# Forget heads' bias by a running sum on VectorE, and 84 matmuls of the unit matrix ahead of the first products

## The chip, the cores and the metric

The kernel runs on one core of one Trainium2 chip. The metric is the time of one execution on the device, in microseconds (us). In what follows PE is TensorE, DVE is VectorE, ACT is ScalarE, POOL is GpSimd and SP is SyncE, whose queue issues most of the DMAs.

## The reference, cut to what matters

One layer mixes 512 tokens of width 2048 through three branches of four heads of 128 channels: A (forgetting attention), B (attention in chunks with a learned bias) and C (stick-breaking attention). Their outputs are gated, projected up, weighted by merge gates, summed and projected out. The change touches branch A:

```python
def forgetting_attention(q, k, v, f_logit):
    log_f = jax.nn.log_sigmoid(f_logit.astype(jnp.float32))
    c = jnp.cumsum(log_f, axis=1).transpose(0, 2, 1)          # (b, heads, tokens)
    for i in range(nb):                                       # blocks of 128 queries
        logits = einsum('bhqd,bhkd->bhqk', q[lo:hi], k[:hi]) * scale
        logits = logits + c[:, :, lo:hi, None] - c[:, :, None, :hi]
        logits = jnp.where(mask, logits, NEG)
        p = jax.nn.softmax(logits, axis=-1)
        outs.append(einsum('bhqk,bhkd->bhqd', p, v[:, :, :hi]))
```

The term `c[query]` is the same for all keys of a row, so a softmax over keys does not depend on it; the term `-c[key]` does matter.

## The kernel before, in words

Activations lie transposed: 128 channels on the partitions, 512 tokens along the row. Every product of float32 operands is made from float32r parts. A weight tile is split by `prep` into a rounded part `wh` (ACT, line 243) and a rest `wl` (DVE, line 247), and `mm` (line 262) multiplies both with the split activations.

The work is a list of units, each one weight tile of 128x1024 (later 128x768). The units come in this order: the first head of branch C through `first_quad`, which takes Q, K, V, G and the forget logits together while x is still being normalised; gate columns; then the heads C1 to C3, B0 to B3, A0 to A3, each with two seven-product tasks for Q/K and V/G and one or two for gate columns; then the up projection (`up_units`) and the output projection (`out_pair`). From the up to the output projection the merged tiles must be combined: `merged_a` and `merged_b` make `m1`, `m2`, `mt`, `mu` and their splits `m23`, `m4` on DVE and ACT.

The order of instructions on PE, ACT and DVE is fixed when the kernel is built. A planner, `Flow`, runs all tasks as generators; each says which engine it wants and for how long, and the planner picks by earliest start and due time. So a task with other costs or other buffers can move instructions of its neighbours. On the chip each engine then works through its own list in order. Weights are fetched by SP (line 274) into six `raw` tiles; sums of weight tiles come by POOL's queue (line 278).

Branch A before. `forget_bias` computes log f of all four heads as a 128x16 tile and stores it to a DRAM tile `fd2`. `forget_sums`, run shortly before A0, loads it four times, makes the running sum over 512 tokens on DVE (`fs`), splits it, and assembles two tiles: `crl` and `crb`, in which rows of the sum and rows of ones stand so that a matmul of the two gives c[query] - c[key]. For each A head, `soft_start` makes `cr` by an ACT copy of `crb` with the mask `ohf` as scale (line 956), and `soft_scores` adds it to the scores in PSUM with one matmul per query block (line 980, 128 to 512 columns). Then a bf16 matmul of the unit matrix `identb` with the mask `mska` adds the causal mask (line 981), DVE takes the maximum (line 984), ACT the exponential straight from PSUM (line 986).

Branch B before. The bias of a head is a tile `tb`, fetched by SP in `soft_start`. DVE adds it to the scores, writes them to SBUF and takes the maximum in one instruction (line 991), reads the maximum out and negates it (line 993); ACT takes the exponential in SBUF (line 996).

At the start of the program PE has nothing to do until x and the first weight tile are loaded and split. `identb` is made early (POOL line 307, DVE line 310).

Of the kernel before, what the change touches and what calls it, by code (L numbers as in the profile page):

```python
# [15 lines left out]
P = 128  # L16
S = 512
# [10 lines left out]
HS = S // 2  # L28
EPS = 1e-6
NEG = -1e30  # L30
SCALE = HD ** -0.5
LA = 2

# [29 lines left out]
class Flow:  # L63
# [16 lines left out]
    def give(self, slots, n=1):  # L80
        slots.free += [self.fin] * n
# [67 lines left out]
def mm_us(n, x=1):  # L149
    return x * max(0.115, n / 2400 + 0.0133)  # L150


def act_us(n, x=1):
    return x * (0.075 + 0.00095 * n)


def dve_us(n, x=1):
    return x * (0.1 + 0.00105 * n)
# [3 lines left out]
def hybrid_kernel(  # L162
# [34 lines left out]
    def t2(s, dt=F32):  # L197
        return tp.tile([P, S], dt, tag="t2", name=nm(s))
# [11 lines left out]
    def f(ap):  # L210
        return ap.bitcast(F32)

    def blk(i):
        return slice(i * P, (i + 1) * P)
# [22 lines left out]
    def pair_of(name, dt=F32R):  # L237
        return t2(name + "h", dt), t2(name + "l", dt)

    def split(hi, lo, src, n, ev=None, due=(), hi_ev=None):  # L240

        yield (ACT, act_us(n), *due)
        nc.scalar.activation(hi, src, AF.Copy)  # L243
        if hi_ev is not None:
            set_(hi_ev)
        yield (DVE, dve_us(n), *due)
        nc.vector.tensor_sub(lo, src, f(hi))  # L247
        if ev is not None:
            set_(ev)
# [23 lines left out]
    def fetch(to, src, ready, kb):  # L273
        nc.sync.dma_start(to, src)
        return Event(landing(ready, kb))
# [42 lines left out]
    nc.gpsimd.affine_select(out=mskc, in_=zerof, pattern=[[-1, P]], base=0, channel_multiplier=1,  # L318
                            compare_op=ALU.is_gt, fill=NEG)

    ohf = cp.tile([P, NH], F32, name="ohf")
    nc.gpsimd.memset(ohf, 0.0)
    for r in range(4):
        nc.gpsimd.affine_select(out=ohf[32 * r:32 * r + 32, :], in_=ohf[32 * r:32 * r + 32, :],
                                pattern=[[1, NH]], base=0, channel_multiplier=-1,
                                compare_op=ALU.not_equal, fill=1.0)

    gq = cp.tile([P, 4], F32, name="gq")
    nc.vector.tensor_copy(gq, gqk)
    for c in (0, 2):  # L330
# [16 lines left out]
    def at(u, g):  # L347
        side.setdefault(u, []).append(g)
# [56 lines left out]
    xraw, x_in = [None] * KT, [Event() for _ in range(KT)]  # L405
    first_ps = att()
    atts.free.pop()
    xps.free.clear()


# [383 lines left out]

    gl = {}
    yd = {}
    bias, bias_ev, f_ev, f2_ev = {}, Event(), Event(), Event()
    fd, fd2 = dp.tile([2 * NH, S], F32, name="fd"), dp.tile([NH, S], F32, name="fd2")

    def forget_bias():  # L800

        T = S // 32
        lf = cp.tile([P, 4 * T], F32, name="lf")
        v, u, s, p = (lf[:, i * T:(i + 1) * T] for i in range(4))
        yield f_ev
        nc.sync.dma_start(v, fd[:NH, :].rearrange("h (c t) -> (h c) t", t=T))
        nc.sync.dma_start(u, fd[NH:, :].rearrange("h (c t) -> (h c) t", t=T))
        yield Event(f_ev.t + 6.0)
        q = 0.15
        yield DVE, q  # L810
        nc.vector.scalar_tensor_tensor(v, v, bfc, u, op0=ALU.add, op1=ALU.add)
        yield DVE, q
        nc.vector.scalar_tensor_tensor(u, v, -1.0, v, op0=ALU.mult, op1=ALU.min)
        yield ACT, q
        nc.scalar.activation(u, u, AF.Exp)

        yield DVE, 5 * q
        nc.vector.tensor_scalar_add(s, u, 2.0)
        nc.vector.reciprocal(s, s)
        nc.vector.tensor_mul(s, s, u)  # L820
        nc.vector.tensor_mul(u, s, s)
        nc.vector.tensor_scalar_mul(p, u, 1.0 / 17.0)
        for k in range(7, 0, -1):
            yield DVE, q
            nc.vector.scalar_tensor_tensor(p, p, 1.0 / (2 * k + 1), u, op0=ALU.add, op1=ALU.mult)
        yield DVE, 3 * q
        nc.vector.scalar_tensor_tensor(p, p, 1.0, s, op0=ALU.add, op1=ALU.mult)
        nc.vector.tensor_scalar_mul(p, p, 2.0)
        nc.vector.scalar_tensor_tensor(v, v, 0.0, p, op0=ALU.min, op1=ALU.subtract)
        nc.sync.dma_start(fd2.rearrange("h (c t) -> (h c) t", t=T), v)  # L830
        f2_ev.t = flow.fin + 3.0

    def forget_sums():
        yield f2_ev
        yield t2s, 3
        v, s, u = t2("fv"), t2("fs"), t2("fu")
        nc.gpsimd.memset(v, 0.0)
        nc.gpsimd.memset(u, 1.0)
        for r in range(4):
            nc.sync.dma_start(v[32 * r:32 * r + NH, :], fd2)  # L840
        yield Event(flow.now + 6.0)
        yield DVE, 1.2
        nc.vector.tensor_tensor_scan(s, u, v, 0.0, op0=ALU.mult, op1=ALU.add)
        give(t2s)
        yield t2s, 2
        hi, lo = pair_of("c")
        yield from split(hi, lo, s, S)
        give(t2s)
        yield t2s, 2
        crl, crb = t2("crl", F32R), t2("crb")  # L850
        a = ACT, act_us(S)
        yield a
        nc.scalar.activation(crl[0:32, :], f(hi[0:32, :]), AF.Copy)
        yield a
        nc.scalar.activation(crl[32:64, :], f(lo[32:64, :]), AF.Copy)
        yield a
        nc.scalar.activation(crl[64:128, :], u[64:128, :], AF.Copy)
        nc.gpsimd.memset(crb[0:64, :], 1.0)
        yield a
        nc.scalar.activation(crb[64:96, :], f(hi[64:96, :]), AF.Copy, scale=-1.0)  # L860
        yield a
        nc.scalar.activation(crb[96:128, :], f(lo[96:128, :]), AF.Copy, scale=-1.0)
        give(t2s, 3)
        bias["crl"], bias["crb"] = crl, crb
        set_(bias_ev)

    def tri(name, dt=F32):

# [5 lines left out]
    class Head:  # L874
# [73 lines left out]
        def soft_start(self):  # L948
            n = self.n
            yield from self.turn()  # L950
            yield t2s, 4
            if n == A:
                yield bias_ev
                self.bias = t2("cr", F32R)
                yield ACT, act_us(S)
                nc.scalar.activation(self.bias, bias["crb"], AF.Copy, scale=ohf[:, self.h:self.h + 1])
                set_(self.event("b"))
            else:
                self.bias = t2("tb")
                ev = fetch(self.bias, rel[self.h], flow.now, 256)  # L960
                yield ev
                yield DVE, 0.15
                nc.vector.memset(self.bias[0:64, S - 64:], NEG)
                set_(self.event("b"))
            self.p = tri("p")[::-1]

        def soft_scores(self, i):
            n = self.n
            m = (i + 1) * P
            for e in (("p", Q), ("p", K), ("b",)):  # L970
                yield self.event(*e)
            yield atts, 1
            (qh, ql), (kh, kl) = self.c[Q], self.c[K]
            yield PE, mm_us(m, 3) + (mm_us(m) + mm_us(P) if n == A else 0)
            ps = att()[:, :m]
            mm3(ps, qh[:, blk(i)], ql[:, blk(i)], kh[:, :m], kl[:, :m], True, n == B)
            p = self.p[i]
            mx, sm = small("mx"), small("sm")
            if n == A:
                nc.tensor.matmul(ps, bias["crl"][:, blk(i)], self.bias[:, :m], start=False, stop=False)  # L980
                nc.tensor.matmul(ps[:, blk(i)], identb, mska, start=False, stop=True)
                done = self.nth("s", QB)
                yield DVE, dve_us(m)
                nc.vector.tensor_reduce(mx, ps, axis=AX.X, op=ALU.max, negate=True)
                yield ACT, act_us(m) + 0.25
                nc.scalar.activation(p, ps, AF.Exp, bias=mx, accum_out=sm)
                give(atts)
            else:
                done = self.nth("s", QB)
                yield DVE, dve_us(m) + 0.15  # L990
                nc.vector.tensor_tensor_reduce(out=p, in0=ps, in1=self.bias[:, S - m:], scale=1.0,
                                               scalar=-3e38, op0=ALU.add, op1=ALU.max, accum_out=mx)
                nc.vector.tensor_scalar_mul(mx, mx, -1.0)
                give(atts)
                yield ACT, act_us(m) + 0.25
                nc.scalar.activation(p, p, AF.Exp, bias=mx, accum_out=sm)
            if done:
                give(t2s, 5)
            yield DVE, 0.16
            nc.vector.reciprocal(sm, sm)  # L1000
            yield ACT, act_us(m) + 0.1
            nc.scalar.activation(p, p, AF.Copy, scale=sm)
            set_(self.event("s", i))
# [273 lines left out]

    first_head(C, 0)
    for n, h in [(C, 1), (C, 2), (C, 3)] + [(n, h) for n in (B, A) for h in range(NH)]:
        if (n, h) == (A, 0):  # L1280
            at(len(units) - 4, forget_sums)
        last_head = head(n, h, (n, h) == (A, NH - 1))


# [304 lines left out]
```

## Time and profile before

| | |
|---|---|
| median of 3 runs | 1350.9 us (1350.63 to 1351.42) |
| the profiled execution's own time | 1351.01 us |
| its span, first to last instruction | 1349.3 us, so 1.7 us lie around it |
| busy share of the span | PE 98%, weight load 85%, DVE 82%, ACT 59%, POOL 7% |
| chain that ended last | PE 96%, DVE 3% |

How to read it: the span is cut into the time in which each engine ran something. PE's matmuls overlap, so the time that one takes from its neighbours is read from start to start and not from its own duration. A row of a timeline has the start, the duration, the engine, the line, the operation, out<-in, shapes and a count; a bracket behind it gives the time that the engine was idle before it and what ended that.

### The profile page before, as it was taken

What the parts mean: (1) busy time and instruction counts of PE and PEld (TensorE: products, weight loads), DVE (VectorE), ACT (ScalarE), POOL (GpSimd) and SP (SyncE); (2) the same over time, 40 slices, a digit from 0 to 9 for tenths busy, and PEclk for the clock granted to TensorE, in tenths of its full rate; (3) what the DMA queues carried; (4) which work ended last, traced back from release to release, by engine and by line L of the source; (5) the groups of instructions that cost most, each with busy time, mean ns of one, the idle gap of its engine ahead of it and who ended that gap; (6) DMA issues with size and microseconds to landing.
All of it is one profiled execution on the core that took longest, in us unless ns stands there. A gap on an engine that the chain in (4) does not pass through costs nothing.

```text
span 1349.3 us, 19660 instructions
## 1 busy us (share of the span) xinstructions
PE 1326.0 (98%) x7338; PEld 1149.2 (85%) x7338; DVE 1108.8 (82%) x1589; ACT 797.3 (59%) x1224; POOL 93.5 (7%) x123
## 2 busy tenths in 40 slices
PE   7999999999999999999999999999999999989998
PEld 5788888888888888888888888888888788878887
DVE  5998998978878788787888878878787877898786
ACT  6755756656565576655767557665567645454443
POOL 0000000010000000000110000100000000000000
PEclk9999999999999999999999999999999999989999
DMA  9556766667767677777777777777767655758893
GB/s 327 173 143 157 194 171 181 187 195 194 187 196 202 183 212 183 187 204 183 212 174 190 193 194 196 167 193 186 192 184 250 246 192 179 209 134 245 236 250 89
DMA packets 91055, 262.00 MB, mean 194 GB/s; under 512 B 10168, under 2 KB 16440, under 8 KB 90960
## 3 DMA queue, kind: packets, MB, share of 16 engines
q1 hardware_dynamic: 72384, 201.96, 44.6%
q0 software_dynamic: 14976, 54.53, 24.7%
q10 hardware_dynamic: 3600, 4.26, 0.9%
q8 instruction: 57, 0.93, 0.3%
q14 instruction: 38, 0.31, 0.1%
HBM read 241.03 MB, written 19.69 MB: 193 GB/s over the span
## 4 chain that ended last, share of the span: by engine, by line
PE 96%; DVE 3%; DMA 0%; issue 0%; ACT 0%; SPq 0%; DVEq 0%; ACTq 0%
PE acc L262 82%; PE att L262 8%; PE att L1013 1%; DVE wl L247 1%; DVE m L247 1%; PE att L1116 1%; PE att L258 1%; PE att L1117 1%; PE att L259 1%; PE att L257 1%; PE att L1115 1%; DMA x<-in_xT 0%; PE att L1076 0%; PE att L911 0%; PE att L912 0%
## 5 line engine op out<-in xcount | busy, mean ns | idle before, releaser
L247 DVE TENSOR_TENSOR wl<-raw,wh 128x1024 fp32r<-128x1024 f32 (+1 forms) x412 | 494.2, 1200 | 149.7 <-ACT wh L243 148.8
L243 ACT ACTIVATE wh<-raw 128x1024 fp32r<-128x1024 f32 (+1 forms) x412 | 427.1, 1038 | 149.8 <-PE acc L262 69.5
L262 PE MATMUL acc<-x,wh 128*128 128x512 f32 x1600 | 416.1, 396 | 10.0 <-ACT wh L243 10.0
L262 PEld LDWEIGHTS acc<-x,wh 128*128 128x128 f32 x1600 | 287.0, 189 | 62.0 <-ACT wh L243 10.0
L262 PE MATMUL acc<-t,wh 128*128 128x512 f32 x1056 | 272.7, 395 | 0.2 <-ACT wh L243 0.2
L262 PEld LDWEIGHTS acc<-x,wl 128*128 128x128 f32 x1504 | 210.6, 190 | 18.9
L262 PE MATMUL acc<-x,wl 128*128 128x256 f32 (+1 forms) x1504 | 223.7, 289 | 0.0
L262 PEld LDWEIGHTS acc<-t,wh 128*128 128x128 f32 x1056 | 188.0, 189 | 31.9 <-ACT wh L243 0.4
L262 PEld LDWEIGHTS acc<-t,wl 128*128 128x128 f32 x1056 | 145.0, 190 | 11.0
L262 PE MATMUL acc<-t,wl 128*128 128x256 f32 x1056 | 148.6, 282 | 0.0
L278 POOL DMA_DIRECT2D raw<-in_w_col x88 | 76.1, 865 | 934.7 <-DMA raw<-in_w_col 429.1
L262 PE MATMUL acc<-m,wh 128*128 128x512 f32 x448 | 113.8, 396 | 6.4 <-DVE m L247 6.0
L262 PEld LDWEIGHTS acc<-m,wh 128*128 128x128 f32 x448 | 81.6, 191 | 21.6 <-DVE m L247 6.4
L746 ACT ACTIVATE c<-acc 128x256 f32<-128x256 f32 x50 | 19.2, 384 | 105.4 <-PE acc L262 100.4
L724 ACT ACTIVATE u<-acc 128x512 f32<-128x512 f32 x50 | 29.8, 596 | 66.6 <-PE acc L262 66.5
L262 PE MATMUL att<-y,wh 128*128 128x512 f32 x256 | 66.5, 391 | 1.3 <-DVE y L247 1.3
L262 PEld LDWEIGHTS acc<-m,wl 128*128 128x128 f32 x448 | 61.9, 193 | 5.1 <-DVE wl L247 0.8
L636 DVE TENSOR_TENSOR raw<-raw,raw 128x1024 f32<-128x1024 f32 x52 | 63.5, 1221 | 0.4
L630 DVE TENSOR_TENSOR raw<-raw,raw 128x1024 f32<-128x1024 f32 x52 | 63.4, 1220 | 0.4
L262 PE MATMUL acc<-m,wl 128*128 128x256 f32 x448 | 63.4, 285 | 0.4 <-DVE wl L247 0.4
L707 ACT ACTIVATE v<-acc 128x512 f32<-128x512 f32 x52 | 31.1, 599 | 49.4 <-PE acc L262 46.1
L262 PEld LDWEIGHTS att<-y,wh 128*128 128x128 f32 x256 | 47.9, 188 | 12.2 <-DVE y L247 2.5
(193 smaller groups left out, 1371.9 us busy)
## 6 DMA issues: line engine op xcount, KB each, us to landing
raw<-in_w_col SPq DMA_DIRECT2D x236, 512.0 KB, 4.4
raw<-in_w_col POOLq DMA_DIRECT2D x88, 512.0 KB, 6.4
raw<-in_w_out SPq DMA_DIRECT2D x40, 512.0 KB, 4.4
gl<-c SPq DMA_DIRECT2D x48, 256.0 KB, 2.2
raw<-in_w_up SPq DMA_DIRECT2D x32, 384.0 KB, 3.1
sg<-gl SPq DMA_DIRECT2D x48, 256.0 KB, 5.1
raw<-in_w_out POOLq DMA_DIRECT2D x16, 512.0 KB, 6.8
x<-in_xT SPq DMA_DIRECT2D x16, 256.0 KB, 7.0
```

Of the source, the lines that this page charges most:

```text
L243: nc.scalar.activation(hi, src, AF.Copy)
L247: nc.vector.tensor_sub(lo, src, f(hi))
L257: nc.tensor.matmul(ps, lh, rh, start=start, stop=False, skip_group_check=more)
L258: nc.tensor.matmul(ps, lh, rl, start=False, stop=False, skip_group_check=more)
L259: nc.tensor.matmul(ps, ll, rh, start=False, stop=stop, skip_group_check=more)
L262: nc.tensor.matmul(ps, w, x, start=start, stop=stop, skip_group_check=more)
L278: nc.gpsimd.dma_start(to, src, accum_op=ALU.add)
L630: nc.vector.tensor_add(w[1], w[1], w[5])
L636: nc.vector.tensor_add(w[2], w[2], w[1])
L707: nc.scalar.activation(self.v, ps, AF.Copy)
L724: nc.scalar.activation(self.u, ps, AF.Copy)
L746: nc.scalar.activation(c, ps[:, RH], AF.Copy, scale=-1.0)
```

## The change

It does two things. First, the forget heads take their bias as branch B does. `forget_bias` stores -log f (one more DVE instruction of 128x16); `forget_sums`, the mask `ohf`, the tiles `crl` and `crb` and the matmul of line 980 are gone. Each A head fetches its row of `fd2` to all 128 partitions (256 KB on SP's queue) into `cr`, and DVE makes the running sum in place (128x512). Each query block is then treated as in B: DVE adds the bias, writes to SBUF and takes the maximum; ACT takes the exponential in SBUF. The mask matmul stays. Second, 84 matmuls of `identb` with itself (128x128, bf16) into the PSUM tile `first_ps` stand ahead of the first product; their result is overwritten.

```diff
+WARM = 84
...
-    ohf = cp.tile([P, NH], F32, name="ohf")
-    nc.gpsimd.memset(ohf, 0.0)
-    for r in range(4):
-        nc.gpsimd.affine_select(out=ohf[32 * r:32 * r + 32, :], in_=ohf[32 * r:32 * r + 32, :],
...
     first_ps = att()
     atts.free.pop()
+    for _ in range(WARM):
+        nc.tensor.matmul(first_ps[:, :P], identb, identb, start=True, stop=True)
...
-        nc.vector.scalar_tensor_tensor(v, v, 0.0, p, op0=ALU.min, op1=ALU.subtract)
+        nc.vector.tensor_scalar(v, v, -1.0, 0.0, op0=ALU.mult, op1=ALU.max)
+        nc.vector.tensor_add(v, v, p)
...
-    def forget_sums():
...
             if n == A:
-                yield bias_ev
-                self.bias = t2("cr", F32R)
-                yield ACT, act_us(S)
-                nc.scalar.activation(self.bias, bias["crb"], AF.Copy, scale=ohf[:, self.h:self.h + 1])
+                yield f2_ev
+                b = self.bias = t2("cr")
+                ev = fetch(b, fd2[self.h:self.h + 1, :].to_broadcast([P, S]), flow.now, 256)
+                yield ev
+                yield DVE, dve_us(2 * S)
+                nc.vector.tensor_tensor_scan(b, b, b, 0.0, op0=ALU.add, op1=ALU.max)
...
             if n == A:
-                nc.tensor.matmul(ps, bias["crl"][:, blk(i)], self.bias[:, :m], start=False, stop=False)
                 nc.tensor.matmul(ps[:, blk(i)], identb, mska, start=False, stop=True)
-                done = self.nth("s", QB)
-                yield DVE, dve_us(m)
-                nc.vector.tensor_reduce(mx, ps, axis=AX.X, op=ALU.max, negate=True)
-                yield ACT, act_us(m) + 0.25
-                nc.scalar.activation(p, ps, AF.Exp, bias=mx, accum_out=sm)
-                give(atts)
-            else:
...
+            done = self.nth("s", QB)
+            yield DVE, dve_us(m) + 0.15
+            b = self.bias[:, :m] if n == A else self.bias[:, S - m:]
+            nc.vector.tensor_tensor_reduce(out=p, in0=ps, in1=b, scale=1.0, scalar=-3e38, op0=ALU.add, op1=ALU.max,
+                                           accum_out=mx)
+            nc.vector.tensor_scalar_mul(mx, mx, -1.0)
+            give(atts)
+            yield ACT, act_us(m) + 0.25
+            nc.scalar.activation(p, p, AF.Exp, bias=mx, accum_out=sm)
...
-        if (n, h) == (A, 0):
-            at(len(units) - 4, forget_sums)
```

Line numbers in rows of the changed kernel differ from those of the kernel before: line 247 becomes 248, 253 becomes 254, 262 becomes 263, 1370 becomes 1326 and 1377 becomes 1333.

The planner moves instructions at three places that the prediction speaks of. The first is the start of PE's list; `acc_224`, `att_226` and so on are the PSUM tiles of the first head, `x_2` the first x tile. Before:

```order
L1584 UNCONDITIONAL_BRANCH
L262 MATMUL acc_224<-x_2_126,wh_214 128x512
L262 MATMUL acc_225<-x_2_126,wh_214 128x512
L262 MATMUL att_226<-x_2_126,wh_214 128x512
L262 MATMUL att_227<-x_2_126,wh_214 128x512
L262 MATMUL att_142<-x_2_126,w_121 8x512
```

With the change, where the pair of lines 403 stands 84 times:

```order
L403 LDWEIGHTS identb
L403 MATMUL att_128<-identb 128x128
L263 MATMUL acc_294<-x_2_112,wh_284 128x512
L263 MATMUL acc_295<-x_2_112,wh_284 128x512
L263 MATMUL att_296<-x_2_112,wh_284 128x512
```

The 84 pairs wait for `identb` alone and stand ahead of everything else on PE; what follows is unchanged.

The second place is DVE at the first scores of A0. `qkl` is the rest of the normalised queries or keys, `wl` that of a weight tile, `att_7580` the PSUM tile of the first scores. Before:

```order
L247 TENSOR_TENSOR qkl_7533<-rs_7342,qkh_7532 128x512
L247 TENSOR_TENSOR wl_7549<-raw_7304,wh_7548 128x1024
L984 TENSOR_REDUCE mx_7584<-att_7580 128x1
L247 TENSOR_TENSOR wl_7575<-raw_7378,wh_7574 128x1024
L1000 RECIPROCAL sm_7585<-sm_7585 128x1
```

With the change:

```order
L248 TENSOR_TENSOR qkl_7579<-rs_7391,qkh_7578 128x512
L248 TENSOR_TENSOR wl_7595<-raw_7353,wh_7594 128x1024
L921 SCALAR_TENSOR_TENSOR cr_7562<-cr_7562 128x512
L248 TENSOR_TENSOR wl_7621<-raw_7427,wh_7620 128x1024
L949 ISA p_7631,mx_7650<-att_7646,cr_7562 128x128
L949 ISA mx_7650 128x1
L951 TENSOR_SCALAR mx_7650<-mx_7650 128x1
```

The running sum (line 921) stands where the first maximum stood, and the next weight split is queued behind it; the first scores come one weight split later, on PE six to sixteen matmuls later. In the other A heads it is the same, in A3 the sum stands ahead of the last `qkl`.

The third place is DVE at the end of the up projection, where `sg` are the gated products, `mt` and `mu` the combinations of merged tiles 6 and 14 (numbers 11567 and 11611 before, 11620 and 11621 after), `m` the splits. Before:

```order
L247 TENSOR_TENSOR m_2108_11612<-sg_11379,m_2108_11612 128x2x256
L253 SCALAR_TENSOR_TENSOR mt_11567<-sg_11379,sg_11307 128x256
L1370 TENSOR_TENSOR sg_11463<-att_11596,sg_11463 128x512
L1377 TENSOR_TENSOR sg_11449<-sg_11449,sg_11463 128x512
L247 TENSOR_TENSOR wl_11620<-raw_11469,wh_11619 128x1024
L253 SCALAR_TENSOR_TENSOR mt_11567<-mt_11567,sg_11307 128x256
L630 TENSOR_TENSOR raw_11469<-raw_11469,raw_11432 128x1024
L1370 TENSOR_TENSOR sg_11518<-acc_11621,sg_11518 128x512
L1396 TENSOR_TENSOR sg_11449<-sg_11449 128x256
L253 SCALAR_TENSOR_TENSOR mu_11611<-mt_11567,sg_11379 128x256
```

With the change:

```order
L248 TENSOR_TENSOR m_2095_11622<-sg_11432,m_2095_11622 128x2x256
L1326 TENSOR_TENSOR sg_11502<-acc_11610,sg_11502 128x512
L254 SCALAR_TENSOR_TENSOR mt_11620<-sg_11432,sg_11360 128x256
L254 SCALAR_TENSOR_TENSOR mt_11620<-mt_11620,sg_11360 128x256
L254 SCALAR_TENSOR_TENSOR mu_11621<-mt_11620,sg_11432 128x256
L248 TENSOR_TENSOR wl_11647<-raw_11449,wh_11646 128x768
L1326 TENSOR_TENSOR sg_11504<-att_11635,sg_11504 128x512
L1333 TENSOR_TENSOR sg_11502<-sg_11502,sg_11504 128x512
L1326 TENSOR_TENSOR sg_11506<-att_11657,sg_11506 128x512
L1333 TENSOR_TENSOR sg_11502<-sg_11502,sg_11506 128x512
```

The three combinations `mt`, `mt`, `mu` now stand together and earlier: all three are ahead of the last two `sg` of that block, where before only the first was. The instructions between there and the last `m23` split are otherwise the same.

More of the change, by code (lines that the diff above doesn't have):

```diff
@@ L319, in hybrid_kernel @@
                             compare_op=ALU.is_gt, fill=NEG)
-    ohf = cp.tile([P, NH], F32, name="ohf")
-    nc.gpsimd.memset(ohf, 0.0)
-    for r in range(4):
-        nc.gpsimd.affine_select(out=ohf[32 * r:32 * r + 32, :], in_=ohf[32 * r:32 * r + 32, :],
-                                pattern=[[1, NH]], base=0, channel_multiplier=-1,
-                                compare_op=ALU.not_equal, fill=1.0)
     gq = cp.tile([P, 4], F32, name="gq")
@@ L796, in hybrid_kernel @@
     yd = {}
-    bias, bias_ev, f_ev, f2_ev = {}, Event(), Event(), Event()
+    f_ev, f2_ev = Event(), Event()
     fd, fd2 = dp.tile([2 * NH, S], F32, name="fd"), dp.tile([NH, S], F32, name="fd2")
@@ L825, in forget_bias @@
             nc.vector.scalar_tensor_tensor(p, p, 1.0 / (2 * k + 1), u, op0=ALU.add, op1=ALU.mult)
-        yield DVE, 3 * q
+        yield DVE, 4 * q
         nc.vector.scalar_tensor_tensor(p, p, 1.0, s, op0=ALU.add, op1=ALU.mult)
         nc.vector.tensor_scalar_mul(p, p, 2.0)
-        nc.vector.scalar_tensor_tensor(v, v, 0.0, p, op0=ALU.min, op1=ALU.subtract)
+        nc.vector.tensor_scalar(v, v, -1.0, 0.0, op0=ALU.mult, op1=ALU.max)
+        nc.vector.tensor_add(v, v, p)
         nc.sync.dma_start(fd2.rearrange("h (c t) -> (h c) t", t=T), v)
         f2_ev.t = flow.fin + 3.0
-    def forget_sums():
[L834 to L865, printed above, removed]
     def tri(name, dt=F32):
@@ L973, in soft_scores @@
             (qh, ql), (kh, kl) = self.c[Q], self.c[K]
-            yield PE, mm_us(m, 3) + (mm_us(m) + mm_us(P) if n == A else 0)
+            yield PE, mm_us(m, 3) + (mm_us(P) if n == A else 0)
             ps = att()[:, :m]
@@ L979, in soft_scores @@
             if n == A:
-                nc.tensor.matmul(ps, bias["crl"][:, blk(i)], self.bias[:, :m], start=False, stop=False)
                 nc.tensor.matmul(ps[:, blk(i)], identb, mska, start=False, stop=True)
-                done = self.nth("s", QB)
-                yield DVE, dve_us(m)
-                nc.vector.tensor_reduce(mx, ps, axis=AX.X, op=ALU.max, negate=True)
-                yield ACT, act_us(m) + 0.25
-                nc.scalar.activation(p, ps, AF.Exp, bias=mx, accum_out=sm)
-                give(atts)
-            else:
[L989 to L996, printed above, removed]
+            done = self.nth("s", QB)
[7 more added lines that the diff above has]
+            nc.scalar.activation(p, p, AF.Exp, bias=mx, accum_out=sm)
             if done:
```

## Prediction

> **What bounds the kernel now.** I read the page's first and fourth part, then PE's waits, then the chain, then the timeline where the change acts.
>
> ```profile
> PE 1326.0 (98%) x7338; PEld 1149.2 (85%) x7338; DVE 1108.8 (82%) x1589; ACT 797.3 (59%) x1224; POOL 93.5 (7%) x123
> ```
> ```profile
> PE 96%; DVE 3%; DMA 0%; issue 0%; ACT 0%; SPq 0%; DVEq 0%; ACTq 0%
> ```
> ```profile
> PE acc L262 <- ACT wh L243: 10.6, 3, 10.0
> PE acc L262 <- DVE m L247: 6.0, 1, 6.0
> PE att L262 <- DVE y L247: 1.3, 2, 1.0
> ```
>
> PE is the bound. It idles 10.0 us before its first matmul, 6.0 us once for a split `m`, 1.3 us for a `y`, and hardly anywhere else. So whatever is taken off PE between the start and the end counts in full, and work on DVE or ACT counts only where PE waits for it. Two windows inside the heads of B and the first of A show the cover:
>
> ```profile
> 539.00:623.00 84.00, 84.00 (x489) 74.02 (x488) 68.78 (x99) 52.64 (x79) 6.91 (x8) 1.00 0.73 193
> 623.00:711.00 88.00, 88.00 (x512) 77.56 (x511) 72.72 (x104) 56.81 (x86) 8.43 (x11) 1.00 0.74 191
> ```
>
> The columns are the length, then the busy time of PE, PEld, DVE, ACT and POOL, the granted clock, the DMA share and GB/s. PE has no idle time in either, DVE is free for 15 us of each.
>
> **Part one, the first products.** PE's first pieces in the chain (start, length, line, count), and what they wait for:
>
> ```profile
> 8.96 0.95 ACT wh L243
> 9.96 1.22 PE acc L262 x2
> 11.19 1.28 PE att L262 x3
> 12.46 0.85 PE acc L262 x2
> 13.32 1.28 PE att L262 x3
> 15.06 0.70 PE att L262 x3
> ```
> ```profile
> 1.66 0.29 DVE L310 CAST identb<-identf 128x128 bf16<-128x128 f32 x1 [0.32 <-POOL identf L307]
> ```
>
> The first ten matmuls of 512 columns run at 1.28/3 = 0.43 us each, later ones at 0.70/3 = 0.23. That is half speed. The page's granted clock says 1.00 there, but the trace has the same picture with the clock beside it after PE's one long wait:
>
> ```profile
> 1195.60:1198.00 2.40, 0.00 (x0) 0.00 (x0) 2.40 (x8) 1.05 (x2) 0.86 (x1) 0.50 0.70 183
> 1198.00:1202.20 4.20, 4.16 (x14) 3.68 (x15) 1.88 (x4) 1.06 (x1) 0.00 (x0) 0.50 0.97 216
> ```
>
> The granted clock is 0.50 while PE idles and for another 4.2 us of work. At the start the slow stretch is as long, from 9.96 to about 14.4. So after some 4.4 us of matmuls the clock is free. If PE has done that before 9.96, the ten matmuls cost 10 x 0.23 and not 10 x 0.43: a gain of 2.0 us. It stays, since PE then runs without a wait to 198 us in this trace, and the DVE's work there follows PE.
>
> What the 84 cost: the nearest rows are the mask matmul of the same type (line 981) and its neighbours.
>
> ```profile
> 756.01 0.28 PE L259 MATMUL att<-qkh,qkl 128*128 128x128 f32 x1
> 756.13 0.27 PE L980 MATMUL att<-cr,crl 128*128 128x128 f32 x1
> 756.24 0.23 PE L981 MATMUL att<-mska,identb 128*128 128x128 bf16 x1
> 756.28 1.40 PE L262 MATMUL acc<-t,wh 128*128 128x512 f32 x5
> ```
> ```profile
> L980 PEld LDWEIGHTS att<-cr,crl 128*128 128x128 f32 x16 | 3.0, 189 | 0.2
> L981 PEld LDWEIGHTS <-identb 128*128 128x128 bf16 x16 | 1.5, 96 | 1.9 <-issue 1.7
> ```
>
> A float32r matmul of 128 columns takes 0.11 us from start to start, the bf16 one 0.04; its weight load lasts half as long (96 against 189 ns). Between 0.04 and 0.11 I take 0.06, half of the float32r one, since weights of 128 columns set that pace and load in half the time. At half clock I double it. `identb` is there at 1.95. In 4.4 slow us 4.4/0.12 = 37 are done, the other 47 take 2.8: the end is at 9.1, before the 9.96 of the first split. At 0.04 it is 7.5; at 0.11 20 are done slowly, 64 take 7.0, and the end is at 13.4: 3.4 us too late, a net loss of 1.4. So this part lies between -2.0 and +1.4, and I take -2.0. [...]
>
> **Part two, the bias matmul.** From the row at 756.13 it costs 0.11 for 128 columns; the other end of its sizes:
>
> ```profile
> 1015.41 0.39 PE L980 MATMUL att<-cr,crl 128*128 128x512 f32 x1
> 1015.64 0.23 PE L981 MATMUL att<-mska,identb 128*128 128x128 bf16 x1
> ```
>
> 0.23 for 512. The sizes 256 and 384 lie between; with 0.12 to 0.15 and 0.17 to 0.19 a head saves 0.63 to 0.68. Four heads: 2.5 to 2.7, I take -2.6. All of it is on PE's path.
>
> What is added for it: per A head one running sum, four reads of the maximum and four negations on DVE, and one DMA on SP. The sum of 512 is priced by the scan of branch C:
>
> ```profile
> L1060 DVE TENSOR_TENSOR_SCAN lk<-lk 128x512 f32<-128x512 f32 x4 | 4.9, 1219 | 0.0
> ```
>
> That is 1.2 us, the reads and negations are what B heads already carry in the window 539 to 623, where 15 us of DVE are free and PE does not idle; so the sum is hidden there, and I cost it at nothing. If that cover were gone it would be 4 x 1.2. The removed `forget_sums` (ACT, DVE, POOL, four DMAs) lies in the window 623 to 711, where PE does not wait either: nothing. The exponential from SBUF instead of PSUM is ACT's, off the path. The mask matmul stays, so its 0.04 stay.
>
> The DMA `cr` adds a wait: DVE's sum waits for its landing, and behind it stand the weight split and the first maximum of that head. Cover: SP issues it where it now issues the gate columns ahead of A0, and the sum stands behind the weight split at 754:
>
> ```profile
> DMA to landing us min/median/max: 6.9/6.9/6.9
> ```
> ```profile
> 742.55 3.53 SPq L1156 DMA_DIRECT2D gl<-c  x2
> ```
> ```profile
> 754.13 1.22 DVE L247 TENSOR_TENSOR wl<-raw,wh 128x1024 fp32r<-128x1024 f32 x1 [0.83 <-ACT wh L243]
> ```
>
> The first row is that of B's `tb`, also 256 KB. Issued at 746.1, `cr` would land at 753.0; DVE gets there at 755.3. That is 2.3 us of room. But each of its 128 rows is the same 2 KB of DRAM, which no row here shows. Bounds: nothing if it takes up to 9 us; if it takes longer DVE stands still, and PE follows once its two split-ahead units (some 6 us) are used up. I cost it at nothing. On SP nothing is pushed back as long as the tile's buffer is free; the next weight there is issued only at 748.7, when a `raw` tile is free.
>
> **Part three, what the planner moved.** PE's wait of 6.0 us before 1198 ends on the last split `m23`, and DVE works through to it from 1171 without a gap:
>
> ```profile
> 1171.19 0.69 DVE L1370 TENSOR_TENSOR sg<-att,sg 128x512 f32<-128x512 f32 x1 [0.36 <-PE att L262]
> 1171.91 0.69 DVE L1377 TENSOR_TENSOR sg<-sg,sg 128x512 f32<-128x512 f32 x1
> 1172.52 1.22 DVE L247 TENSOR_TENSOR wl<-raw,wh 128x1024 fp32r<-128x1024 f32 x1
> 1173.66 0.42 DVE L253 SCALAR_TENSOR_TENSOR mt<-mt,sg 128x256 f32<-128x256 f32 x1
> 1173.99 1.22 DVE L630 TENSOR_TENSOR raw<-raw,raw 128x1024 f32<-128x1024 f32 x1
> ...
> 1176.06 0.42 DVE L253 SCALAR_TENSOR_TENSOR mu<-mt,sg 128x256 f32<-128x256 f32 x1
> 1176.40 1.22 DVE L247 TENSOR_TENSOR wl<-raw,wh 128x1024 fp32r<-128x1024 f32 x1
> ```
> ```profile
> 1167.58 0.96 DVE L247 TENSOR_TENSOR wl<-raw,wh 128x768 fp32r<-128x768 f32 x1 [1.14 <-ACT wh L243]
> ```
>
> The `mt` at 1173.66 and the `mu` at 1176.06 take 0.33 each from start to start. With the change they stand ahead of 1171, where DVE was idle (1.14 before 1167.58). The gapless stretch has 0.7 less to do: -0.7. Bounds: -2.0 if DVE's end moves further by better use of that gap, +1 if the other order makes DVE wait for ACT. The 1.3 us for `y` may move by half a microsecond either way, since the last head's scores come later and its sums earlier; taken as nothing.
>
> **Sum.** -2.0 - 2.6 - 0.7 = -5.3. From the profiled execution's own 1351.0 (span 1349.3 and 1.7 around it) that is 1345.7; the median of the runs is 1350.9, 0.1 lower, which changes nothing. A measurement of this kernel can tell about 0.2%, 2.7 us, from no change: below 1348.2 is faster, above 1353.6 slower.
>
> **Rivals.**
>
> The 84 matmuls last too long. For: a stream of loads and matmuls has no row in this trace. Against: the bf16 load is half as long. The point of decision is an end at 12.0, a pace of 0.09. At 0.11 the sum is +1.4 - 2.6 - 0.7 = -1.9: 1349.1, no change that can be told. Chance 0.13.
>
> The 84 do not free the clock, or the 2.0 us are eaten further on: -3.3, 1347.7. For: unit matrices are mostly zeros, and the page's clock says 1.00 at the start; against: the two stretches at half speed look alike. Chance 0.10. [...]
>
> Slower: `cr` lands late in every A head, because 128 reads of one row of DRAM take their turn. It decides from 15 us (9 of room and some 6 of units split ahead). At 18 us PE waits 3 us four times, +12 - 5.3: 1357.6. Against it: 256 KB in 6.9 us for `tb`. Chance 0.06.
>
> The wait before 1198 falls short enough that the clock is not lost: the 4.2 us of half speed cost about 2, so 1343.6. Against: the clock fell about 3.5 us into it, and 6.0 - 0.7 is still 5.3. Chance 0.08. The remainder, 0.03, goes to a stall that I have not seen.
>
> **Numbers.** Mine 0.60; its own range is 1344.5 to 1347.2. Range for 8 in 10, with the neighbours: 1343.4 to 1349.3. Faster: 0.60 + 0.08 + most of the 0.10 + the easier part of the 0.13 = 0.80. Same 0.13, slower 0.07.
>
> **What would show it.** The matmuls of the unit matrix end before the first product, which starts near 10 and runs at 0.23 at once; the period from an A head to the next is shorter by 0.65; no PE wait for a weight split or a softmax tile in the A heads; the wait for `m` near 5.3 us, still followed by a clock of 0.50. Wrong would make it: a first product after 11, PE idle behind `cr`, a wait for `m` that is longer than 6.

## The result, and the profile after

The changed kernel takes 1346.45 us in the median of 7 runs (1345.91 to 1346.76), the kernel before beside it 1351.04 (1350.51 to 1351.49). The ratio is 0.9966, 95% interval 0.9954 to 0.9978: 4.6 us faster, where 5.3 were forecast. The profiled execution took 1346.45 us, its span is 1344.7.

The page's busy times and its chain, then the idle times of PE (in total, how often, the longest):

```profile
PE 1328.4 (99%) x7406; PEld 1151.6 (86%) x7406; DVE 1112.7 (83%) x1624; ACT 792.7 (59%) x1214; POOL 91.3 (7%) x115
```
```profile
PE 97%; DVE 1%; DMA 0%; ACT 0%; issue 0%; SPq 0%; DVEq 0%; ACTq 0%
```
```profile
PE acc L263 <- DVE m L248: 5.9, 1, 5.9
PE att L403 <- DVE identb L311: 1.9, 1, 1.9
PE acc L263 <- ACT wh L244: 1.4, 2, 1.0
PE att L971 <- ACT p L1023: 1.4, 1, 1.4
PE att L263 <- DVE y L248: 1.3, 2, 1.0
```

The 10.0 us ahead of the first product have become 1.9 for `identb` and about 1 for the first weight split, with the 84 matmuls between. The wait for `m` is 5.9 and not 5.3. The wait for `p`, in the first head of C, is 0.4 longer than before; the leads below show no loss there.

Where did the 4.6 us come from? The transposes of the value tiles stand in every head, four of them each, so the start of their first and last says how much earlier PE is. Before, and with the change (x48: minimum, median and maximum in ns, first and last start):

```profile
L1076 PE MATMUL att<-identf,c x48: 270/272/307, 164.7 to 1028.1; 128*128 128x128 f32 x48
```
```profile
L1034 PE MATMUL att<-identf,c x48: 270/272/298, 162.6 to 1023.5; 128*128 128x128 f32 x48
```

PE is 2.1 us earlier at the first head and 4.6 at the last (4.53 with more digits). In between nothing happens until the A heads: head by head the lead is 2.09, 2.09, 2.08, 2.07 (C), 2.10, 2.10, 2.08, 2.05 (B), then 2.67, 3.29, 3.90, 4.53 (A). The start is worth 2.1 in these two profiles, each A head 0.62, and what follows adds 0.1 up to the end.

The start. A row of this view has the start, the duration, then engine, line and operation:

```profile
1.92 7.06 PE L403 MATMUL att<-identb 128*128 128x128 bf16 x84 [1.92 <-DVE identb L311]
9.94 0.73 PE L263 MATMUL acc<-x,wh 128*128 128x512 f32 x2 [0.96 <-ACT wh L244]
10.50 0.62 PE L263 MATMUL att<-x,wh 128*128 128x512 f32 x2
```

The 84 end at 8.98. The first 43 spacings between them are 0.107 us, the others 0.056. The products start at 9.94, 0.02 earlier than before, and from the second on stand 0.23 apart, where it was 0.43 before.

The first scores of A0 on PE, without the bias matmul, and the new running sum on DVE:

```profile
755.82 0.27 PE L260 MATMUL att<-qkh,qkl 128*128 128x128 f32 x1
755.94 0.23 PE L945 MATMUL att<-mska,identb 128*128 128x128 bf16 x1
755.98 0.48 PE L263 MATMUL acc<-t,wl 128*128 128x256 f32 x2
```
```profile
744.13 0.38 SPq L275 DMA_DIRECT2D cr<-fd  x1
```
```profile
L921 DVE TENSOR_TENSOR_SCAN cr<-cr x4: 1217/1218/1218, 753.2 to 1005.7; 128x512 f32<-128x512 f32 x4
...
DMA to landing us min/median/max: 4.7/6.7/7.0
```
```profile
711.00:1004.00 293.00, 293.00 (x1699) 256.77 (x1698) 244.00 (x337) 183.05 (x272) 24.19 (x28) 1.00 0.72 190
```

`cr` is issued at 744.1 and lands by 751.1 even with the longest of its four times; DVE comes to it at 753.2. In the last row, the window over heads A0 to A3, PE is busy for all 293.00 us.

### The profile page after: what moved, and what is told of

It is laid out like the page before. It is cut to its first block, busy times and chain, and to the rows that moved or that the text cites. A ratio compares the mean times of both kernels' runs of the same rounds, so it can differ in the third digit from the quotient of the medians.

```text
span 1344.7 us, 19813 instructions
## 1 busy us (share of the span) xinstructions
PE 1328.4 (99%) x7406; PEld 1151.6 (86%) x7406; DVE 1112.7 (83%) x1624; ACT 792.7 (59%) x1214; POOL 91.3 (7%) x115
## 4 chain that ended last, share of the span: by engine, by line
PE 97%; DVE 1%; DMA 0%; ACT 0%; issue 0%; SPq 0%; DVEq 0%; ACTq 0%
PE acc L263 84%; PE att L263 9%; PE att L971 1%; PE att L1074 1%; PE att L1075 1%; PE att L259 1%; PE att L260 1%; PE att L258 1%; DVE wl L248 1%; PE att L1073 1%; DMA x<-in_xT 0%; PE att L1034 0%; PE att L875 0%; PE att L874 0%; DVE m L248 0%; ACT wh L244 0%
```

## The experiments

Each kernel was timed in rounds beside the kernel before, whose median was 1351.59 (first four kernels), 1350.69 (next four), 1350.55 (next two) and 1350.98 (last two). Ratios are to that kernel.

**The 84 matmuls alone.**

```diff
 (the kernel before)
+WARM = 84
...
+    for _ in range(WARM):
+        nc.tensor.matmul(first_ps[:, :P], identb, identb, start=True, stop=True)
```

> The kernel before with the 84 matmuls of the unit matrix added and nothing else. My theory (the start is worth 2.0 to 2.1 us, the rest comes from the A heads): 1349.0 us, ratio 0.9985 to the kernel before. Rival (the start's gain is eaten further on and the whole gain comes from the bias): 1351.0, ratio 1.000. Rival (the start carries more than its own part): below 1348.

Measured: 1348.8, ratio 0.9983 (0.9974 to 0.9992). The start alone is faster by 0.8 to 2.6 parts in a thousand. In this profile the lead at the first head is 1.5 and not 2.1. Its start, and a matmul of the normalisation further on:

```profile
2.01 6.12 PE L410 MATMUL att<-identb 128*128 128x128 bf16 x84 [2.01 <-DVE identb L311]
9.88 0.73 PE L263 MATMUL acc<-x,wh 128*128 128x512 f32 x2 [1.75 <-ACT wh L244]
```
```profile
36.24 1.10 PE L473 MATMUL att<-dg,tmpc 128*128 128x512 f32 x2 [0.41 <-ACT dg L469]
```

The same 84 take 6.1 us here and 7.1 in the changed kernel, because only 24 of the spacings are slow and not 43. And some 0.5 us of the gain are lost at 36 us, where PE, now early, waits 0.41 for the tile `dg`, which ACT has not written yet. Far behind, 0.7 come back by no doing of the change: from the matmul that waits for `m` to the seventeenth behind it, where the clock is low (0.50 in the kernel before), it is 4.40 us here and 5.06 in the kernel before. So the 2.2 us by which this profile is shorter are 1.5 and 0.7.

**The bias alone.**

```diff
-WARM = 84
+WARM = 0
```

> The changed kernel without the 84 matmuls. My theory (2.5 us from the four A heads, 0.1 from the up to output transition, first product at half speed as before): 1348.5 us, ratio 0.998. Rival (the moved instructions at the transition give their 0.7 as forecast): 1347.7. Rival (the two parts help each other): the two gains of this run and of the other one do not add up to 4.6.

Measured: 1347.96, ratio 0.9976 (0.9967 to 0.9986), an interval that holds 2.5 us. The leads of its profile grow by 0.62 from one A head to the next, as in the changed kernel. The first products are slow again, 0.43 us apart, and longer than in the kernel before (until about 15.4 us, there until 14.4), so PE is 0.6 us behind that kernel at the first head:

```profile
10.09 1.22 PE L263 MATMUL acc<-x,wh 128*128 128x512 f32 x2 [10.09 <-ACT wh L244]
```

With 1 - 0.9983 and 1 - 0.9976 the two parts sum to 0.0041, against 0.0034 for both: they add up within the intervals. The forecast 0.7 of the transition cannot be told from 0.1 by this time; the trace says it below.

**44 matmuls in place of 84.**

```diff
-WARM = 84
+WARM = 44
```

> The changed kernel with 44 matmuls of the unit matrix in place of 84. They end near 6.6 us, when the slow stretch of 4.6 us is just over, and TensorE then idles for about 3.3 us before the first product. Theory A (4.6 us of work free the clock, and an idle time under about 3.5 us keeps it): first products 0.23 us apart, time as with 84, 1346.4. Theory B (the work must reach up to the first product): first products 0.43 us apart again, 1348.4.

Measured: 1348.25, ratio 0.9976 (0.9967 to 0.9986): as without any. But neither theory is right as it stands:

```profile
1.92 4.87 PE L403 MATMUL att<-identb 128*128 128x128 bf16 x44 [1.92 <-DVE identb L311]
9.88 0.74 PE L263 MATMUL acc<-x,wh 128*128 128x512 f32 x2 [3.08 <-ACT wh L244]
10.46 0.70 PE L263 MATMUL att<-x,wh 128*128 128x512 f32 x2
10.95 0.63 PE L263 MATMUL att<-x,w 128*8 128x512 f32 x1
11.37 1.06 PE L263 MATMUL acc<-x,wh 128*128 128x512 f32 x2
```
```profile
10.00:14.40 4.40, 4.40 (x13) 3.17 (x14) 4.26 (x6) 3.77 (x8) 0.00 (x0) 0.61 1.06 385
```

The clock was free at first: up to the start of the fifth product it is 1.07 us (9.88 to 10.95), in the changed kernel 1.03 and in the kernel before 1.88. From 10.95 to about 14 they stand 0.43 apart, so the clock fell at about 10.9, after PE had idled for 3.08 us and then worked again for 1. The second fence is a window from 10.0 to 14.4, with a granted clock of 0.61.

**140 matmuls.**

```diff
-WARM = 84
+WARM = 140
```

> The changed kernel with 140 matmuls of the unit matrix in place of 84. At 0.056 us each the further 56 end near 12.0 us instead of 9.0. My theory (a late first product counts in full, and only the part behind 9.94 is late): first product at 12.0, time 1346.4 + 2.1 = 1348.5. Rival (later waits take the delay up): 1346.5.

Measured: 1348.61, ratio 0.998 (0.9971 to 0.9989).

```profile
1.92 10.76 PE L403 MATMUL att<-identb 128*128 128x128 bf16 x140 [1.92 <-DVE identb L311]
12.49 0.70 PE L263 MATMUL acc<-x,wh 128*128 128x512 f32 x2
```

The first product is 2.55 us late, and the lead at the first head goes from 2.09 to -0.44: at the start all of the delay counts, as the first rival of the prediction had it. The expectation had the start 0.5 too early (12.0) and yet the time right. In the profiled execution 0.6 of the 2.5 us come back behind the wait for `m`, where the seventeen matmuls take 4.51 us and in the changed kernel 5.15.

**64 matmuls.**

```diff
-WARM = 84
+WARM = 64
```

> The changed kernel with 64 matmuls of the unit matrix in place of 84. They end between 7 and 8.3 us, so TensorE idles for 1.6 to 3 us before the first product, less than the 3.1 us after which the run with 44 lost its clock. Theory A (an idle stretch below about 3 us keeps the clock): first products at 0.23 us throughout, 1346.4. [...]

Measured: 1346.05, ratio 0.9966 (0.9952 to 0.9979), and a lead of 2.17 at the first head.

```profile
9.83 0.74 PE L263 MATMUL acc<-x,wh 128*128 128x512 f32 x2 [2.66 <-ACT wh L244]
```

An idle stretch of 2.66 us kept the clock in this profile (from the second on the products stand 0.23 apart), and none of the five times (1345.68 to 1346.23) shows a loss. 64 do what 84 do.

**The changed kernel again, a filler in the wait for `m`, and the order of DVE at that wait.** For the filler, the order and the second running sum further down the base is the changed kernel in the same rounds: 

> The changed kernel as it is, for a base on the same chip and in the same rounds as the three beside it. All theories: 0.9966 of the kernel before, about 1346.5 us.

Measured: 1346.24, ratio 0.9967 (0.9955 to 0.998).

The filler, in `mms_of`, ahead of the eighth matmul of product 6 in the first output pair:

```diff
+                        for _ in range(70):
+                            nc.tensor.matmul(fill[:, :P], identb, identb, start=True, stop=True)
                     yield ev
```

> The changed kernel with 70 further matmuls of the unit matrix in TensorE's list just ahead of the matmul that waits 5.9 us for the last split m23. At 0.056 us each they take 3.9 us and leave about 2 us of the wait idle, so the operand is still what ends it. My theory (only the idle time drops the clock): the clock stays at 1.00 behind the wait, the matmuls of 512 columns there go from 0.43 to 0.23 us each, the time is 1.9 to 2.1 us below the changed kernel. Rival (unit matrices do not hold the clock, or the clock falls for another reason): no difference.

Measured: 1344.73, ratio 0.996 (0.9947 to 0.9974), 1.5 us under the base. In the changed kernel and with the filler:

```profile
1193.38 0.80 PE L263 MATMUL acc<-m,wh 128*128 128x512 f32 x1 [5.87 <-DVE m L248]
...
1198.53 1.11 PE L263 MATMUL acc<-m,wl 128*128 128x256 f32 x8
```
```profile
1187.58 4.08 PE L666 MATMUL att<-identb 128*128 128x128 bf16 x70
1193.61 0.50 PE L264 MATMUL acc<-m,wh 128*128 128x512 f32 x1 [1.94 <-DVE m L249]
...
1196.74 1.11 PE L264 MATMUL acc<-m,wl 128*128 128x256 f32 x8
```

From the waiting matmul to the last row shown it is 5.15 us in the first and 3.13 in the second: the clock, granted at 0.50 from 1193 to 1196 in the first and at 1.00 in the second, costs 2.0 there. The theory holds in the profile. Two of the five times (1346.19 and 1346.41) show no gain, and the mean granted clock of these two is 0.999, of the other three 1.000 and of the base 0.997: by that the clock was not at 1.00 throughout in these two. Where it fell is open.

**`m23` ahead of `mu`.**

```diff
 (merged_b, for k == 7 alone)
-        minus(u, t[:, LH], b[:, LH])
         yield up_done
...
-        yield from split(m23[k].hi, m23[k].lo, two(t), S, ev, (due + 7.0,))
+        yield from split(m23[k].hi, m23[k].lo, two(t), S, ev, (due + 0.0,))
+        minus(u, t[:, LH], b[:, LH])
```

> The changed kernel in which the last merged_b makes its split m23 before its mu, with an earlier due time, so that on VectorE the split stands right behind the sum of line 751 and no longer behind seven instructions for m4, mu and a weight split (4.4 us). My theory (the order of VectorE's list at this place, and not the amount of its work, sets the wait): the wait for m falls from 5.9 to about 1.2 us, a wait of about 1 us for the last m4 may follow, the clock is kept (2 us); 1340.6 us, between 1339.5 and 1343. Rival (VectorE's amount of work sets it and the wait only moves to the m4 splits or a weight split): total waits as before, 1346.4.

Measured: 1342.94, ratio 0.9944 (0.9931 to 0.9956), 3.3 us under the base and not 5.6. DVE first in the changed kernel, then with the new order, where the split follows the sum of line 751 at once:

```profile
1187.09 0.69 DVE L751 TENSOR_TENSOR t<-v,acc 128x512 f32<-128x512 f32 x1
...
1192.63 0.70 DVE L248 TENSOR_TENSOR m<-mt,m 128x512 fp32r<-128x512 f32 x1
```
```profile
1187.65 0.68 DVE L248 TENSOR_TENSOR m<-mt,m 128x512 fp32r<-128x512 f32 x1
```
```profile
1188.39 0.50 PE L263 MATMUL acc<-m,wh 128*128 128x512 f32 x1 [0.91 <-DVE m L248]
...
1194.88 0.50 PE L263 MATMUL acc<-m,wh 128*128 128x512 f32 x1 [0.63 <-DVE m L248]
...
1202.70 2.14 PE L263 MATMUL acc<-m,wh 128*128 128x512 f32 x8 [0.79 <-ACT wh L244]
1207.02 1.25 PE L263 MATMUL acc<-m,wl 128*128 128x256 f32 x8 [2.19 <-DVE wl L248]
1208.08 3.57 PE L263 MATMUL acc<-m,wh 128*128 128x512 f32 x8
```

The split moved by 5.0 us and the wait fell from 5.87 to 0.91. But PE, now early, waits 0.63 for the last `m4`, 0.79 for a `wh` and 2.19 for a `wl` of the second pair. The eight matmuls behind that take 3.57 us and not 2.00: in this execution the clock was lost after all (0.81 granted from 1205 to 1210). In sum, PE is 7.0 us ahead of the changed kernel once the wait for `m` and the slow stretch behind it are past (5.0 from the wait, 2.0 from the clock). The three new waits take 4.4 of it (3.6 idle, 0.8 at the restarts), the lost clock 1.6, and 1.4 come back near the end, where two waits of the changed kernel (0.44 and 0.40) are gone. That leaves 2.4 in this execution, which took 1344.06; one that keeps the clock would be 1.6 shorter.

**A filler in the new wait, and earlier sums of weights.** Both start from the kernel with `m23` ahead of `mu`.

```diff
 (product 6 of the second output pair, ahead of its wl)
+                    for _ in range(28):
+                        nc.tensor.matmul(fill[:, :P], identb, identb, start=True, stop=True)
```

> The kernel with m23 ahead of mu, and 28 matmuls of the unit matrix (1.6 us) in TensorE's list just ahead of its new wait of 2.2 us for a weight split in the second output pair. My theory (of the 5.8 us forecast for the order alone, 1.6 us were lost because the clock fell behind this new wait): eight matmuls of 512 columns behind it at 0.23 us instead of 0.43, 1.5 us less than without the 28, 1341.4. Rival (the clock there falls by the whole idle time of the stretch, 0.8 us ahead of it included, or the 28 make the split's wait longer): 1342.9.

Measured: 1342.57, ratio 0.9938 (0.9926 to 0.9951). In its profile the wait is 0.64 and the eight matmuls behind it take 2.00, so the clock was kept (1.00 granted from 1205 to 1210); the five times lie at 1342.41 to 1342.85. The forecast of 1341.4 was missed.

```diff
-                spawn(self.task.sums(), 3.0)
+                spawn(self.task.sums(), 0.5 if self.task.rest is not None else 3.0)
```

> The kernel with m23 ahead of mu, and with the sums of two weight tiles in the output pairs due 0.5 us after their operands and not 3 us, so that on VectorE the first sum of the second pair and the split that TensorE waits for stand three to five instructions earlier. My theory (the gain of the order is given back at the next places where VectorE's list has a weight behind other work): the waits of 0.8 and 2.2 us in the second pair fall below 1 us in sum and the clock is kept, 1342.9 - 2.2 - 1.6 = 1339.1. Rival (the weights come too late from memory, and no order of VectorE helps): 1342.9.

Measured: 1342.33, ratio 0.9941 (0.9927 to 0.9954). The wait and what follows it:

```profile
1206.86 1.21 PE L263 MATMUL acc<-m,wl 128*128 128x256 f32 x8 [2.08 <-DVE wl L248]
1207.91 2.00 PE L263 MATMUL acc<-m,wh 128*128 128x512 f32 x8
```

The theory of the second kernel failed: the wait is still 2.08, since the sums only changed places with other work of a DVE that has no gap there. Yet the eight matmuls behind it take 2.00, and the granted clock is 1.00. Nearly the same idle times that cost the clock in one execution (0.79 and 2.19) did not in another (0.77 and 2.08). So the 1.5 us of the filler cannot be read from the medians: without it three of the five times of the kernel with `m23` ahead of `mu` lie at 1342.44 to 1342.94 (granted clock 0.999 to 1.000) and two at 1344.02 and 1344.06 (0.998). Against the last two the filler is worth 1.5 us, against the other three nothing; that it always keeps the clock is not shown by five times. All three kernels beat the kernel before and the changed kernel; which of them is the fastest stays open.

**A second running sum.** (`twice` is the tile `cr` in A heads.)

```diff
             self.p = tri("p")[::-1]
+            if twice is not None:
+                nc.vector.tensor_tensor_scan(self.p[3], twice, twice, 0.0, op0=ALU.add, op1=ALU.max)
```

> The changed kernel with a second running sum of 128x512 on VectorE in each of the four A heads, written to a tile that is overwritten later. My theory (VectorE's running sum is hidden): the same time as the changed kernel, within 0.5 us. Rival (it is on the path, and so the first one is too): 4 x 1.22 = 4.9 us more, 1351.3. In between: about 1.2 us for the first head alone.

Measured: 1346.28, ratio 0.997 (0.9959 to 0.9981), against 1346.24 for the base. In A0:

```profile
753.13 1.22 DVE L921 TENSOR_TENSOR_SCAN cr<-cr 128x512 f32<-128x512 f32 x1
754.39 1.22 DVE L934 TENSOR_TENSOR_SCAN p<-cr 128x512 f32<-128x512 f32 x1
```

The second sum is as hidden as the first; only at A3 does the lead fall behind the changed kernel's trend, by 0.2 us.

**DVE with 1.13 us less to do.** The edit is in the first output pair, and the product there lacks one sum of weight tiles:

```diff
-            nc.vector.tensor_add(w[2], w[2], w[1])
```

> The changed kernel without one instruction of VectorE: the second sum of two weight tiles in the first output pair (1.13 us from start to start) is left out, so that the product there takes a weight tile that is not summed; order and all else stay. Theory A (behind 1174.8 VectorE has no gap, so work taken off it there shortens the wait for the last m23 by about as much): the wait falls from 5.9 to about 4.9 us, 1345.4. Theory B (the chain of the trace is right that the sum of line 751 follows a matmul of TensorE that ends at 1187.08): the wait stays at 5.9, 1346.4.

Measured: 1346.31, ratio 0.9968 (0.9955 to 0.998), no gain in the time; in the profiled execution, the slowest of the five with 1347.28, the lead at the first head was only 0.7, so the place itself is the measure.

```profile
1184.55 0.69 DVE L713 TENSOR_TENSOR t<-u,acc 128x512 f32<-128x512 f32 x1 [0.72 <-PE acc L263]
```
```profile
1194.46 0.80 PE L263 MATMUL acc<-m,wh 128*128 128x512 f32 x1 [5.53 <-DVE m L248]
```

Of the 1.13 us, 0.72 came back at once as a wait of DVE for PE's third product, and the wait for `m` fell by 0.34. Both theories are wrong: A in its size, B in that the wait moved at all. The 0.34 can be read from the changed kernel's own trace. PE and DVE stand there at

```profile
1181.99 1.12 PE L263 MATMUL acc<-m,wl 128*128 128x256 f32 x8
...
1183.48 0.68 DVE L712 TENSOR_TENSOR t<-u,acc 128x512 f32<-128x512 f32 x1
```

With the sum left out the same matmuls of PE start at 1183.40, 1.41 us later, and let DVE go on at 1184.55. In the changed kernel, where they end at 1183.11, they would let it go on at 1183.14, and DVE comes at 1183.48. It was 0.34 us behind its operand, and so much could be won.

## Why the prediction was right, point by point

**Part one** (-2.0, measured -2.1). The pace and the doubling while slow came out as worked out: 0.056 and 0.107 us, 43 slow spacings where 37 matmuls were reckoned. That the weight load sets this pace was the author's estimate: no run took the load apart from the matmul. That the end came so near the 9.1 (8.98) is in part luck: the slow stretch, taken as 4.4 us from two rows, was 2.6 to 5.1 us in the nine profiles with 84, and the end lay at 8.13 to 9.28. All of it is ahead of the first product, so the gain did not hang on it. The gain itself is one draw: the products without the 84 were slow until 14.4 us in one profile and until about 15.4 in another. Whether unit matrices free the clock was the rival at 0.10; they do: the spacing of 0.43 us at the start became 0.23. The places that could take the gain back were not named in the prediction. In two of the ten profiles that have a gain at the start PE waited 0.4 us for `dg` at 36 us, in one of these also 0.3 for a weight split at 30 us, and the lead was 1.5 (the 84 alone) and 0.7 (the kernel with a sum left out) instead of about 2.1.

**Part two** (-2.6, measured -2.5). Each head gave 0.62; the sum of four bias matmuls of 128 to 512 columns was taken as 0.65. All the covers held: `cr` landed with 2 us to spare, PE did not idle in the A heads, and even two running sums cost nothing that the times can tell.

**Part three** (-0.7, measured -0.1). This is the term that was mis-sized. The step "the gapless stretch has 0.7 less to do" was wrong: DVE has less to do there, but PE does not let it begin the rest much sooner. `mt` and `mu` did move ahead, and at the front of the stretch DVE then waited for PE's last up products. Before, then with the change:

```profile
1178.24 1.07 PE L262 MATMUL att<-y,wl 128*128 128x512 f32 x4
...
1179.46 0.69 DVE L1370 TENSOR_TENSOR sg<-att,sg 128x512 f32<-128x512 f32 x1
```
```profile
1166.64 0.69 DVE L1326 TENSOR_TENSOR sg<-att,sg 128x512 f32<-128x512 f32 x1 [1.18 <-PE att L263]
...
1173.69 1.07 PE L263 MATMUL att<-y,wl 128*128 128x512 f32 x4
...
1174.80 0.69 DVE L1326 TENSOR_TENSOR sg<-att,sg 128x512 f32<-128x512 f32 x1 [0.47 <-PE att L263]
```

With the change the stretch without a gap begins at 1174.80, when PE lets it. The same matmuls of PE stood 4.55 us later before (1178.24 and 1173.69), so PE would have let DVE go on at 1179.35, and DVE came at 1179.46. It was 0.11 us behind PE at that instruction, and no work taken off ahead of it could win more. From there to the last split DVE needs the same in both, 17.84 and 17.83 us (to 1197.30 and to 1192.63), although one `mt` has moved ahead in that part too. This agrees with the wait for `m`: it is 5.97 and 5.98 us in the two profiles with the old bias, and 5.86 to 5.87 in the seven profiles with the new one and nothing else changed at this place.

Two runs show the same rule from the other side. 1.13 us less in the middle of the stretch gave 0.34, which is what DVE was behind its operand at the sum of line 712. The new order behind the sum of line 751, where no operand of PE stood between, gave 5.0. So the length of the stretch does not tell what can be won; the time by which DVE comes later than PE's operand does. The rest of that part held: the wait for `y` stayed at 1.3, and the granted clock behind the wait for `m` was 0.50 (the number ahead of the last two):

```profile
1193.00:1196.00 3.00, 2.62 (x10) 2.52 (x11) 0.74 (x3) 1.06 (x1) 0.00 (x0) 0.50 0.63 149
```

2.1 + 2.5 + 0.1 is 4.7, against 4.6 measured; the other 0.1 is the slow stretch behind the wait, where the seventeen matmuls take 5.15 us and took 5.06 before. Of the 0.7 us that the forecast had too much, part three is 0.6.

## What to carry to other kernels

An engine that shows no gap ahead of a wait is not therefore its cause in full. Look at each of its instructions there that takes an operand from the other engine, and at how long that operand had been ready: work taken off ahead of it wins no more than that, here 0.11 and 0.34 us of 0.67 and 1.13. Where a wait ends on one late operand, the place of that one operand in its engine's list can be worth more than work taken off the list, here 5.0 us of the wait. A stretch of cheap matmuls ahead of the first product paid here when it ended before the first operand was there and at most 2.66 us ahead of it; 3.08 us lost the clock, and nothing between was run.

## What the runs showed of the hardware

The slow stretch at the start is not a fixed time. With the same list up to there, the slow spacings of 0.107 us were 24 (2.6 us) in the kernel with the 84 alone, 43 (4.6) in the changed kernel, 54 (5.8) with 140: a spread of 3.2 us. Behind the wait for `m` it is the same: the seventeen matmuls take 4.40 to 5.71 us in the ten profiles in which that wait is 5.5 to 6.0 us and stays idle, and 3.13 where the filler kept the clock. So two profiles of such kernels can differ by a microsecond there with nothing changed. What sets the length of the slow stretch no run shows. The slow clock came back after one idle stretch of 3.08 us with 1 us of work behind it, and in one of two executions with nearly the same idle times, after 0.79 and 2.19 us with 2.1 us of work between them; one idle stretch of 2.66 us kept the free clock.

The granted clock of the profile reads 1.00 while PE runs at half speed at the start (1.00 from 1.9 to 6.5 in the changed kernel; 0.107 us there and then 0.056 for the same matmul), and 0.50 or 0.61 in later slow stretches. At the start it is the spacing that tells.
